# A series of 552 TensorE matmuls behind the last store of a one-layer decoder step

## The chip, the cores and the metric

The kernel runs on one core of a Trainium2 chip. The metric is the device time of one execution in microseconds (us). A program has five queues that matter here: TensorE (PE, with its weight loads shown apart as PEld), VectorE (DVE), ScalarE (ACT), GpSimd (POOL) and SyncE (SP). SP issues nearly all DMA transfers; ACT and POOL issue some.

## The reference, cut to what matters

One layer of a hybrid decoder is computed for 256 prompt tokens and 8 sample tokens, so 264 token columns in all, with a model width of 2048:

```
z  = rmsnorm(x) @ w_in                    # RG-LRU group and mLSTM group from one projection
x  = x + concat(y_rg, y_ml) @ w_out
x  = x + cross_attention(rmsnorm(x), memory K/V)
x  = x + (silu(xf @ w_gate) * (xf @ w_up)) @ w_down
y  = rmsnorm_final(x)
```

The outputs are y, the new recurrent states and the memory keys and values. All is float32.

## The kernel before

The token columns lie along the free axis (`N = 264`) and the model width along the partitions, in 16 chunks of 128 (`KC = 16`). A list `steps` holds the projections one after the other. For each step the weights are fetched by SP into a tile `raw` (128 x 1024), split by ACT and DVE into a high and a low part in float32r (tiles with the tag `w`, four buffers of `WW = 2176` columns), and multiplied on TensorE. Each product of 128 x 128 weights with 128 x 264 activations takes three matmuls (`mm3`: high by high, high by low, low by high), so that float32 accuracy comes from float32r matmuls. Their moving operands lie in tiles with the tag `B`, and every moving operand in the kernel is read over consecutive columns. The memory keys and values use 512- and 256-column matmuls of the same type. A few small matmuls (token sums, spreading a column, transposes) are done in plain float32; the profile shows each of those as two rows.

The activations in flight belong to generators that a planner advances between steps by estimated clocks; the order on SP is written out by hand, that of the other engines is set by a scheduler. None of that order is touched ahead of the final normalisation.

The end of the kernel is what the change and the prediction speak of. After the last down projection the sum of squares goes over DVE, ACT and PE; `rstd_fin` leaves the factor twice, once in a PSUM bank (read by DVE) and once copied by ACT into the tile `rstd` (read by POOL). Then 16 chunks of `y` are multiplied, 12 on DVE and the four of `POOLC = (4, 5, 10, 11)` on POOL, and stored in nine transfers, four issued by ACT and five by SP:

```python
    for lo, hi in ((0, 1), (1, 2), (2, 4), (4, 6), (6, 8), (8, 10), (10, 12), (12, 14), (14, 16)):
        for c in range(lo, hi):
            e, r = (pool_e, rstd) if c in POOLC else (dve, fin["ps"][:, :N])
            e.tensor_mul(st["y"](c), st["y"](c), r)
        (act if lo in (1, 4, 8, 12) else sp).dma_start(o_y[:, lo:hi, :], st["y"].tile(lo // 4)[:, lo % 4: lo % 4 + hi - lo, :])
```

`st["y"].tile(q)` is one of four `B` tiles that hold four chunks each. A PSUM tile (`bank()`) has 512 float32 columns. After these lines each queue waits at a barrier for the others, SP also for the landing of the stores, and the execution ends.

## Time and profile before

| | us |
|---|---|
| two timed runs | 1552.85 and 1553.53, median 1553.19 |
| span of the profiled execution, first to last instruction | 1548.1 |
| PE busy | 1533.5 (99%), 12098 instructions |
| PEld busy | 1500.4 (97%) |
| DVE busy | 1055.5 (68%) |
| ACT busy | 784.0 (51%) |
| mean granted TensorE clock | 0.997 |

The profile gives the span of the execution that it recorded; the time of a run contains what lies around the span, and the median is 5.1 us above it. The duration of one matmul in the profile is a latency: matmuls overlap, so that what one of them costs in a stream is the distance from one start to the next, which is got from a stretch of time and the number of matmuls in it.

### The profile page before, as it was taken

Reading aid. Unit: us, or ns where it says so; the run is one execution under the profiler, and the core shown is the slowest. Engines: PE = TensorE matmul, PEld = TensorE weight load, DVE = VectorE, ACT = ScalarE, POOL = GpSimd, SP = SyncE. Lnnn points to the kernel's source line nnn. Section 1 sums busy time; section 2 is a strip of 40 time slices with the busy share of each in tenths; the row PEclk is TensorE's granted clock in tenths of the full one; section 3 lists DMA queues with packets and bytes.
Section 4 is the critical chain, followed back from the end, with each engine's and each line's share of the span. In section 5 each row is a group of like instructions: output and inputs, shape, how many; then the busy total and the mean of one; then the engine's idle time right before and its main releaser. Section 6 shows DMA issues by size and latency. Waiting matters only on the chain.

```text
span 1548.1 us, 30188 instructions
## 1 busy us (share of the span) xinstructions
PE 1533.5 (99%) x12098; PEld 1500.4 (97%) x12098; DVE 1055.5 (68%) x2026; ACT 784.0 (51%) x1255; POOL 123.7 (8%) x190
## 2 busy tenths in 40 slices
PE   9999999999999999999999999999999999999997
PEld 9999999999999888899999999999999999999997
DVE  7886888796699989876665555445555545555554
ACT  7565775665455656555444444333444433444463
POOL 0001210000134333310000000000000000000000
PEclk9999999999999999999999999999999999999999
DMA  9556984547789887855555555555555555555563
GB/s 301 187 164 204 309 288 171 193 158 259 251 294 356 320 296 252 309 181 180 187 177 181 186 181 188 181 185 183 183 185 181 186 183 186 180 188 178 163 181 107
DMA packets 99757, 326.01 MB, mean 211 GB/s; under 512 B 10945, under 2 KB 19825, under 8 KB 99617
## 3 DMA queue, kind: packets, MB, share of 16 engines
q1 hardware_dynamic: 83472, 269.57, 52.1%
q0 software_dynamic: 15136, 53.16, 9.7%
q8 instruction: 94, 1.54, 0.4%
q10 hardware_dynamic: 1008, 1.36, 0.3%
q14 instruction: 47, 0.38, 0.1%
HBM read 312.78 MB, written 11.28 MB: 209 GB/s over the span
## 4 chain that ended last, share of the span: by engine, by line
PE 96%; DVE 2%; ACT 1%; DMA 0%; issue 0%; SPq 0%; DVEq 0%; ACTq 0%
PE mm L60 90%; PE ax L60 6%; DVE B L60 1%; ACT B L60 0%; DVE w L60 0%; DMA raw<-w_in 0%; ACT w L60 0%; ACT L60 0%; DVE xres L60 0%; DVE c L60 0%; ACT rstd L60 0%; SPq L1278 0%; DVE acc_x L60 0%; DVEq L1429 0%; ACT t L60 0%
## 5 line engine op out<-in xcount | busy, mean ns | idle before, releaser
L60 PE MATMUL mm<-B,w 128*128 128x264 f32 (+1 forms) x10960 | 1365.3, 285 | 4.1 <-DVE w L60 2.4
L60 PEld LDWEIGHTS mm<-B,w 128*128 128x128 f32 x10960 | 1338.6, 188 | 16.4 <-DVE w L60 2.8
L60 ACT ACTIVATE w<-raw 128x1024 fp32r<-128x1024 f32 (+1 forms) x522 | 537.9, 1031 | 654.6 <-PE mm L60 447.3
L60 DVE TENSOR_TENSOR w<-raw,w 128x1024 fp32r<-128x1024 f32 (+1 forms) x522 | 623.1, 1195 | 357.0 <-ACT w L60 356.0
L60 PE MATMUL mm<-w,B 128*128 128x512 f32 x384 | 91.0, 391 | 0.0
L60 PEld LDWEIGHTS mm<-w,B 128*128 128x128 f32 x384 | 70.7, 188 | 14.3
L60 DVE TENSOR_TENSOR t<-mm,rstd 128x264 f32<-128x264 f32 x104 | 44.8, 431 | 44.2 <-PE mm L60 43.5
L1344 POOL TENSOR_TENSOR B<-B,rstd 128x264 f32<-128x264 f32 x4 | 2.8, 736 | 855.5 <-ACT rstd L60 855.5
L60 DVE TENSOR_TENSOR xres<-xres,mm 128x264 f32<-128x264 f32 (+1 forms) x81 | 34.2, 423 | 38.9 <-PE mm L60 38.9
L60 DVE SCALAR_TENSOR_TENSOR B<-B,dw 128x256 f32<-128x256 f32 x128 | 55.6, 488 | 3.9 <-ACT dw L60 3.9
L60 DVE SCALAR_TENSOR_TENSOR dw<-B,qsm,dw 128x256 f32<-128x256 f32 x96 | 49.6, 525 | 0.4
L60 PE MATMUL ax<-B,B 128*128 128x256 f32 (+3 forms) x288 | 48.1, 308 | 0.0
L60 PEld LDWEIGHTS ax<-B,B 128*128 128x128 f32 x288 | 40.8, 190 | 3.2 <-ACT w L60 0.3
L1031 POOL TENSOR_TENSOR ds<-dw,ds 128x256 fp32r<-128x256 f32 x32 | 34.6, 1085 | 108.1 <-ACT ds L60 108.1
L60 ACT ACTIVATE B<-xres,vecs 128x264 fp32r<-128x264 f32 (+1 forms) x64 | 32.1, 502 | 1.5 <-DVE xres L60 1.0
L60 ACT ACTIVATE t<-xres 128x264 f32<-128x264 f32 (+2 forms) x61 | 24.0, 410 | 15.2 <-DVE xres L60 15.2
L1020 POOL DMA_DIRECT2D B<-kcT x32 | 17.3, 542 | 140.1 <-DVE B L60 131.0
L60 ACT ACTIVATE B<-t 128x264 fp32r<-128x264 f32 (+1 forms) x60 | 24.2, 409 | 4.6 <-DVE t L60 4.3
L60 DVE TENSOR_TENSOR acc_x<-acc_x,t 128x264 f32<-128x264 f32 x59 | 25.1, 426 | 1.0 <-ACT t L60 0.5
L60 DVE SCALAR_TENSOR_TENSOR B<-xres,vecs,B 128x264 fp32r<-128x264 f32 x48 | 23.4, 487 | 3.1 <-ACT B L60 3.1
L60 ACT ACTIVATE t<-t 128x264 f32<-128x264 f32 (+1 forms) x61 | 24.8, 406 | 1.3 <-DVE t L60 1.2
L60 ACT ACTIVATE dw<-B,qsm 128x256 f32<-128x256 f32 x32 | 16.2, 507 | 17.4 <-DVE B L60 10.7
(152 smaller groups left out, 666.9 us busy)
## 6 DMA issues: line engine op xcount, KB each, us to landing
raw<-w_gu SPq DMA_DIRECT2D x176, 512.0 KB, 3.5
raw<-w_d SPq DMA_DIRECT2D x80, 512.0 KB, 3.5
raw<-w_in SPq DMA_DIRECT2D x74, 512.0 KB, 4.6
raw<-w_out SPq DMA_DIRECT2D x32, 512.0 KB, 4.0
B<-kcT POOLq DMA_DIRECT2D x32, 512.0 KB, 8.1
raw<-w_q SPq DMA_DIRECT2D x32, 512.0 KB, 3.7
B<-vcT POOLq DMA_DIRECT2D x32, 512.0 KB, 8.5
raw<-w_k SPq DMA_DIRECT2D x32, 512.0 KB, 6.8
```

Source lines behind the costliest of these rows:

```text
L60: return f(*a, **k)
L1020: pool_e.dma_start(kc, kcT[h, b])
L1031: pool_e.tensor_sub(ws[:, 1], acc, ws[:, 0].bitcast(F32))
L1344: e.tensor_mul(st["y"](c), st["y"](c), r)
```

## The change

A function `probes` is added and called after the last store. It copies chunks of the finished `y` with ACT into three tiles of the tag `w`, and then lets TensorE run 23 forms of 24 matmuls each, 552 in all, with weights from the first tile (eight places in turn) and a moving operand from the second. The results go to one PSUM bank that nothing reads. The third tile is written and never read.

```diff
+    def probes(y):
+        RL = 24
+        wt = [sb.tile([P, WW], F32R, tag="w", bufs=4, name=nm("w")) for _ in range(3)]
+        for n, t in enumerate(wt):
+            for q in range(2):
+                act.activation(t[:, q * 1056: q * 1056 + 1056].rearrange("p (c n) -> p c n", n=N), y.tile(q + n % 2), AF.Copy)
+            act.activation(t[:, 2112:2176], y.tile(n)[:, 0, 0:64], AF.Copy)
+        banks = [bank() for _ in range(2)]
+        mm = nc.tensor.matmul
+        W_ = lambda k: wt[0][:, 264 * (k % 8): 264 * (k % 8) + P]
+        with tc.manual_schedule(engines={mybir.EngineType.PE}):
+            N2, W2 = [[1, 132], [132, 2]], [[1, 256], [256, 2]]
+            A2, E2 = [[2, 132], [1, 2]], [[2, 256], [1, 2]]
+            pat = [
+                ("plain", 0, [[1, 264]], None), ("plain", 0, [[1, 264]], None),
+                ("halves in turn, out plain", 0, N2, [[1, 264]]),
+                ("halves in turn, out by pairs", 0, N2, A2),
+                ("pairs, out plain", 0, A2, [[1, 264]]), ("pairs, out by pairs", 0, A2, A2),
+                ("backward pairs", 1, [[2, 132], [-1, 2]], [[1, 264]]),
+                ("halves in turn from 4", 4, N2, [[1, 264]]), ("halves in turn from 2", 2, N2, [[1, 264]]), ("halves in turn from 8", 8, N2, [[1, 264]]),
+                ("512 plain", 0, [[1, 512]], None), ("512 halves in turn, out plain", 0, W2, [[1, 512]]),
+                ("512 pairs", 0, E2, E2),
+                ("512 lines in turn", 0, [[1, 256], [1056, 2]], [[1, 512]]),
+                ("256 plain", 0, [[1, 256]], None), ("256 halves in turn", 0, [[1, 128], [128, 2]], [[1, 256]]),
+                ("128 plain", 0, [[1, 128]], None), ("128 halves in turn", 0, [[1, 64], [64, 2]], [[1, 128]]),
+                ("backward halves in turn", 131, [[-1, 132], [132, 2]], [[1, 264]]),
+                ("second half first", 132, [[1, 132], [-132, 2]], [[1, 264]]),
+                ("512 halves in turn in two groups", 0, [[256, 2], [1, 128], [128, 2]], [[1, 512]]),
+                ("two far lines in turn, 512", 0, [[1, 256], [1024, 2]], [[1, 512]]),
+                ("plain", 0, [[1, 264]], None),
+            ]
...
+            for name, o, ap, oap in pat:
+                x = AP(wt[1][:, o: o + 1], ap)
...
+                for k in range(RL):
+                    mm(out, W_(k), x, start=k == 0, stop=k == RL - 1, skip_group_check=True)
...
+    probes(st["y"])
```

A pattern is a list of pairs of a step and a count in columns of 4 bytes, the last pair running fastest: `[[1, 132], [132, 2]]` reads columns 0, 132, 1, 133, 2, 134 and so on, two streams in turn. The moving operand of a "pairs" form names its columns two by two, which is their plain order. All outputs are written to consecutive columns.

On TensorE the program ended with the spreading of the final factor (`ident` by the column `c`, into the bank `ax`); now the series follows it. `mm_17856` is the bank, `w_17845` the moving tile and `w_17844` the weights. The piece of TensorE's difference at the end of the program:

```order
 L60 MATMUL ax_17814<-ident,c_17798 128x128 x2
 L60 MATMUL ax_17814<-ident,c_17798 128x8
-L1429 UNCONDITIONAL_BRANCH
+L957 MATMUL mm_17856<-w_17845,w_17844 128x264 x240
+L957 MATMUL mm_17856<-w_17845,w_17844 128x512 x96
+L957 MATMUL mm_17856<-w_17845,w_17844 128x256 x48
+L957 MATMUL mm_17856<-w_17845,w_17844 128x128 x48
+L957 MATMUL mm_17856<-w_17845,w_17844 128x264 x48
+L957 MATMUL mm_17856<-w_17845,w_17844 128x512 x48
+L957 MATMUL mm_17856<-w_17845,w_17844 128x264 x24
+L1478 UNCONDITIONAL_BRANCH
```

Nothing on TensorE ahead of the series moved; 552 matmuls stand behind what used to be its last. The first of them waits for ACT's copies.

On ACT, the end of the program before, from the last small activation on (`B_17017`, `B_17227`, `B_17436` and `B_17645` are the four tiles of `y`):

```order
L60 ACTIVATE c_17798<-c_17797 128x3
L60 ACTIVATE rstd<-ax_17814 128x264
L1345 DMA o_y<-B_17017 128x264
L1345 DMA o_y<-B_17227 128x528
L1345 DMA o_y<-B_17436 128x528
L1345 DMA o_y<-B_17645 128x528
L1429 UNCONDITIONAL_BRANCH
```

And the same place with the change, up to the copy for which the first matmul of the series waits:

```order
L60 ACTIVATE c_17798<-c_17797 128x3
L60 ACTIVATE w_17844<-B_17017 128x64
L60 ACTIVATE rstd<-ax_17814 128x264
L1392 DMA o_y<-B_17017 128x264
L60 ACTIVATE w_17844<-B_17017 128x1056
L60 ACTIVATE w_17845<-B_17227 128x64
L1392 DMA o_y<-B_17227 128x528
L1392 DMA o_y<-B_17436 128x528
L1392 DMA o_y<-B_17645 128x528
L60 ACTIVATE w_17844<-B_17227 128x1056
L60 ACTIVATE w_17845<-B_17227 128x1056
```

One 64-column copy stands ahead of the copy of `rstd`, a 1056-column and a 64-column copy stand between ACT's first and second store, and the other copies behind ACT's last store. The first matmul of the series waits for the last row shown; behind it ACT has four more copies (`w_17845<-B_17436` and three into the third tile). DVE, POOL and SP keep their order.

More of the change, by code (lines that the diff above doesn't have):

```diff
@@ L907, in layer_kernel, with AP @@
         proj(w_in[33 + j], rx, evac_o(j))
+    def probes(y):
[20 more added lines that the diff above has]
+                ("512 pairs", 0, E2, E2),
[3 rows of a table added]
+                ("backward halves in turn", 131, [[-1, 132], [132, 2]], [[1, 264]]),
[4 more added lines that the diff above has]
+            ]
+            def AP(src, ap):
+                return bass.AP(src.tensor, src.offset, [list(src.ap[0])] + [list(q) for q in ap])
+            for name, o, ap, oap in pat:
+                x = AP(wt[1][:, o: o + 1], ap)
+                out = AP(banks[0][:, 0: 1], oap or ap)
+                if len(ap) == 2 and oap is not None and len(oap) == 1:
+                    out = AP(banks[0][:, 0: 1], oap).rearrange("p (a b) -> p a b", b=ap[-1][1])
+                if len(ap) == 3:
+                    out = banks[0].rearrange("p (a b c) -> p a b c", a=2, c=2)
+                for k in range(RL):
+                    mm(out, W_(k), x, start=k == 0, stop=k == RL - 1, skip_group_check=True)
```

## The prediction

> **What bounds the kernel now.** I read the shares by engine first, then the chain that ended last, then the end of the timeline.

> ```profile
> span 1548.1 us, 30188 instructions
> PE 1533.5 (99%) x12098; PEld 1500.4 (97%) x12098; DVE 1055.5 (68%) x2026; ACT 784.0 (51%) x1255; POOL 123.7 (8%) x190
> PE 96%; DVE 2%; ACT 1%; DMA 0%; issue 0%; SPq 0%; DVEq 0%; ACTq 0%
> ```

> TensorE sets the time of all stages but the last few microseconds. The change touches only that end, so the end is what has to be read:

> ```profile
> 1538.24 1.50 PE L60 MATMUL ax<-ident,c 128*128 128x128 f32 x12
> 1539.12 4.16 DVE L60 TENSOR_TENSOR B<-B,ax 128x264 f32<-128x264 f32 x12 [0.93 <-PE ax L60]
> 1539.57 4.73 SPq L1345 DMA_DIRECT2D o_y<-B  x5
> 1539.92 3.21 ACTq L1345 DMA_DIRECT2D o_y<-B  x4
> 1540.26 2.84 POOL L1344 TENSOR_TENSOR B<-B,rstd 128x264 f32<-128x264 f32 x4 [855.47 <-ACT rstd L60]
> o_y<-B SPq DMA_DIRECT2D x4, 264.0 KB, 2.6
> ```

> TensorE has its last work at 1538.24 and is done at 1539.74. DVE multiplies `y` until 1543.28, POOL until 1543.10, ACT has issued its stores by 1543.13 and SP its last one by 1544.30; with 2.6 us to landing that is 1546.9, and the span ends 1.2 us after it, the closing of the program. So 8 us of TensorE idleness stand at the end, and only stores run there.

> **The change part by part.** *What is added ahead of the series: ACT's copies.* The first matmul waits for the second 1056-column copy behind ACT's last store. Copies of nearly that width:

> ```profile
> L60 ACT ACTIVATE w<-raw 128x1024 fp32r<-128x1024 f32 x36 | 38.2, 1060 | 47.1 <-PE mm L60 19.8 <-issue 18.4 <-ACT B L60 8.8
> ```

> 1060 ns for 1024 columns makes 1.09 us for 1056 columns. ACT is free at 1543.13 as before: the copies put between its stores (one of 1056, two of 64 columns) fit into the time in which it waits for DVE and POOL, 1540.2 to 1542.6, so I cost them at nothing; without that cover they would cost 1.09 us and some 0.3 each for the small ones. The 64-column copy ahead of `rstd` holds up POOL by at most 0.3 us and with it SP's last two stores, which land long before the series ends; if POOL were late enough to hold up ACT's stores too, the series would start by as much later. Two copies from 1543.13 on bring **the first matmul at 1545.3**. At that moment the stores are still landing, and the four copies left on ACT (3 x 1.09 and a small one, until some 1549) run beside the series.

> *The series.* It has 144 matmuls of 264 columns read in plain order (three plain forms, two by pairs, one by backward pairs, which takes each pair of neighbours together), 48 of 512, 24 of 256 and 24 of 128 read so; and, read as two streams in turn, 168 of 264, 96 of 512, 24 of 256 and 24 of 128 columns. Plain pitches:

> ```profile
> 900.00:1000.00 100.00, 100.00 (x837) 100.00 (x836) 54.86 (x64) 40.27 (x46) 0.00 (x0) 1.00 0.55 185
> 566.91 5.40 PE L60 MATMUL mm<-w,B 128*128 128x512 f32 x23
> 589.25 1.12 PE L60 MATMUL ax<-B,B 128*128 128x256 f32 x8
> 1535.24 0.83 PE L60 MATMUL mm<-ones 128*128 128x128 f32 x6
> 1535.12 0.76 PEld L60 LDWEIGHTS mm<-ones 128*128 128x128 f32 x6
> ```

> The first row is 100 us of the down and up projections, all 264-column matmuls: 100 / 837 = 0.120 us each. In the others I take the latency of the last matmul off (means in the row groups below) and divide by the steps between starts: (5.40 - 0.39) / 22 = 0.228 us for 512 columns, (1.12 - 0.28) / 7 = 0.120 for 256, (0.83 - 0.27) / 5 = 0.112 for 128. The last agrees with the weight load, (0.76 - 0.19) / 5 = 0.114: a matmul of 128 columns is bound by its weights.

> ```profile
> L60 PE MATMUL mm<-w,B 128*128 128x512 f32 x384 | 91.0, 391 | 0.0
> L60 PE MATMUL ax<-B,B 128*128 128x256 f32 x216 | 33.9, 295 | 0.0
> L60 PE MATMUL mm<-B,w 128*128 128x264 f32 x10448 | 1272.4, 283 | 4.1 <-DVE w L60 2.4 <-DVE B L60 1.7
> ```

> Plain forms: 144 x 0.120 + 48 x 0.228 + 24 x 0.120 + 24 x 0.112 = **33.8 us**.

> [...]

> *The forms in turn* have no row: no matmul of the kernel before reads its moving operand with a step. Below stands the plain pitch, as if the order of reading cost nothing. Above I look for the slowest stream of columns in the trace, the plain float32 product, which is shown as two rows per matmul:

> ```profile
> 75.91 1.05 PE L60 MATMUL ax<-B,B 128*128 128x264 f32 x4
> L60 PE MATMUL ax<-B,B 128*128 128x264 f32 x32 | 8.4, 386 | 0.0
> ```

> (1.05 - 0.39) / 3 = 0.222 us for one row of 264 columns, two clock steps per column, and 0.444 for the product of two rows. These are my three prices per 264 columns: 0.120 below, 0.222 in the middle, 0.444 above. I take the middle one. A plain read finds the next column beside the last one, and a read in turn finds it 256 to 4224 bytes away every time; if the operand is fetched by more than one column at once, half of what is fetched is lost at the least, and two steps per column is the smallest whole number above one. In proportion to the columns: 168 x 0.222 + 96 x 0.431 + 24 x 0.215 + 24 x 0.112 (two steps for 128 columns just equal the weight load) = 37.3 + 41.3 + 5.2 + 2.7 = **86.5 us**. The backward pairs would add 24 x 0.102 = 2.4 us if they too went by halves.

> [...]

> *The clock.* After TensorE's last work the granted clock goes down, and it comes back in steps of 3.41 us:

> ```profile
> 122.31:125.72 3.41, 3.41 (x18) 3.41 (x17) 3.41 (x5) 0.30 (x2) 0.00 (x0) 0.50 0.60 185
> 1542.10:1542.25 0.15, 0.00 (x0) 0.00 (x0) 0.15 (x2) 0.00 (x0) 0.15 (x1) 1.00 1.18 437
> 1542.26:1548.00 5.74, 0.00 (x0) 0.00 (x0) 1.01 (x3) 0.00 (x0) 0.84 (x2) 0.50 0.72 275
> ```

> The drops at 122.31 and 1542.25 lie 416 x 3.413 us apart, as on a fixed grid. The next points of it are 1545.7 and 1549.1. The series starts inside the first of these intervals, so the full clock is back at 1549.1, after one wholly busy interval. From 1545.3 to 1549.1 half the work is done: **1.9 us** lost.

> *The end.* Behind the last matmul come its latency beyond its pitch (0.16 us) and the closing, 1.2 us as before: **1.4 us**. The stores have long landed.

> **Sum.** 1545.3 + 33.8 + 86.5 + 1.9 + 1.4 = 1668.9 us of span. The time lies 5.1 us above the span (1553.2 against 1548.1), so **1674 us**, +121 us or 7.8%. Nothing ahead of 1540 us is changed: the order on PE, DVE, POOL and SP is the same there.

> **The rivals.**

> *Reading in turn costs nothing.* The forms in turn go at the plain pitch: 168 x 0.120 + 96 x 0.228 + 24 x 0.120 + 24 x 0.112 = 47.7 us in place of 86.5, so 1674 - 38.8 = 1635 us. For it: in the plain rows TensorE takes 4 bytes per column at every step, and the 2.40 columns per ns between the 256- and the 512-column pitch ((512 - 256) / (0.228 - 0.120) = 2370 per us) show no limit of the fetch other than the array's own step. Against it: all these rows are of neighbours.

> *Only some addresses collide.* Streams 132 columns (528 bytes) apart go at the plain pitch, streams a multiple of 256 bytes apart at half of it: the 168 matmuls of 264 columns cost 20.2 us, the rest 49.2 as above, together 69.4: 1657 us. For it: the plain pitch is not quite even, and the kernel's tables lay weights and activations at fixed distances. Against it: no row here separates addresses.

> *Every column waits for its own fetch, four steps.* With 0.444 us per 264 columns: 74.6 + 82.7 + 10.3 + 5.2 = 172.8 us, so 1674 + 86.3 = 1760 us. For it: if one fetch brings four neighbouring columns, a read in turn uses a quarter of it. Against it: nothing in the trace streams that slowly.

> *The series is not run, or runs inside the end.* The results are unread, and every form begins anew in the same bank; if the matmuls were dropped ahead of execution, only ACT's copies would remain: five of 1.09 us and a small one from 1543.13 on, 1548.9, closing 1.2: span 1550.1, time 1555 us, within 2%. It decides from the point where 552 matmuls take less than 1548.1 + 31 - 1545.3 - 1.4 = 32 us, 59 ns each. Against it: the program's order for TensorE holds all 552, each with its own weights, and the trace has no pitch below the 0.112 of a weight load for any full-width matmul.

> **How the numbers follow.** A difference of 2% (31 us) is about what a measurement of this kernel can tell from no change. Chances: two steps per column 0.40, no cost 0.21, some addresses 0.13, four steps 0.22, not run 0.02, anything else 0.02. The ends of the unknown price are the first rival at 1635 and the four steps at 1760. Each holds about a fifth, so that neither can be left out together with the last two cases. With a few us for the uneven plain pitch the range is 1630 to 1765. All cases but one are slower by over 2%: slower 0.98, same 0.02, faster 0.

> **What would show it.** In the changed profile: the first matmul of line 957 at 1545.3 (right if within 0.7 us), behind a copy on ACT; a granted clock of 0.50 until 1549.1 and 1.00 after; the rows of the plain forms at 0.120 and 0.228 us; those in turn at 0.222 and 0.431 with 0.215 and 0.112 for the narrow ones; the backward pairs at 0.120; and 1.4 us between the last matmul's start and the end. The forecast is wrong if the forms in turn stand at any other pitch, or differ among each other; if plain forms in this layout (weights and moving operand in two like tiles) are slower than in the projections, the first term is mis-sized; and if TensorE is slower ahead of 1540 us, the change reaches further than I read it.

## The result, and the profile after

| | before | with the series |
|---|---|---|
| time, median | 1553.19 us | 1632.4 us (1631.46 and 1633.34) |
| ratio | | 1.0515 (95% interval 1.0496 to 1.0535) |
| span of the profiled execution | 1548.1 us | 1631.6 us |

The kernel is slower by 79 us, inside the range and in the direction forecast, but 42 us below the likeliest value. What happened is the first rival (1635 us), and a little more than it: reading two streams in turn does not cost twice the plain pitch, as the forecast had it; it is quicker than plain reading (0.1125 us for 264 columns against 0.121).

The page of the changed kernel; the last two rows are groups (line, engine, operation, count, busy time, mean latency, idle time before):

```profile
span 1631.6 us, 31303 instructions
PE 1616.7 (99%) x12650; PEld 1578.1 (97%) x12650; DVE 1055.1 (65%) x2026; ACT 790.3 (48%) x1264; POOL 125.1 (8%) x190
L957 PE MATMUL mm<-w,w 128*128 128x264 f32 (+3 forms) x552 | 80.7, 310 | 5.5 <-ACT w L60 5.5
L957 PEld LDWEIGHTS mm<-w,w 128*128 128x128 f32 x552 | 75.8, 192 | 10.4 <-ACT w L60 5.6
```

All 552 matmuls ran, so the case that they are dropped is out; together they took 80.7 us. The end of the timeline:

```profile
1542.55 1.50 PE L60 MATMUL ax<-ident,c 128*128 128x128 f32 x12
1543.42 4.17 DVE L60 TENSOR_TENSOR B<-B,ax 128x264 f32<-128x264 f32 x12 [0.93 <-PE ax L60]
1544.90 1.23 ACT L60 ACTIVATE w<-B 128x1056 fp32r<-128x1056 f32 x2 [0.42 <-DVE B L60]
1546.03 1.39 ACTq L1392 DMA_DIRECT2D o_y<-B  x3
1547.47 5.12 ACT L60 ACTIVATE w<-B 128x1056 fp32r<-128x1056 f32 x6 [1.34 <-POOL B L1391]
1549.58 80.74 PE L957 MATMUL mm<-w,w 128*128 128x264 f32 x552 [5.53 <-ACT w L60]
```

The first matmul of the series starts 7.03 us (1549.58 - 1542.55) after the first `ident` matmul; 7.06 had been forecast (1545.3 - 1538.24). It waits for ACT, as the row says.

Stretches of the series, each from the first matmul of one form to the first of the next (start and end, length, then busy time and count of PE, PEld, DVE, ACT, POOL, then the granted clock; the counts include the matmuls cut by the edges, 24 start in each). In order: the first plain form, the second, halves in turn, pairs, backward pairs, 512 plain, 512 halves in turn, 256 plain, 256 halves in turn:

```profile
1549.58:1553.92 4.34, 4.34 (x25) 4.34 (x25) 0.00 (x0) 3.02 (x4) 0.00 (x0) 0.66 0.26 94
1553.92:1556.82 2.90, 2.90 (x27) 2.90 (x25) 0.00 (x0) 0.00 (x0) 0.00 (x0) 1.00 0.00 0
1556.82:1559.52 2.70, 2.70 (x27) 2.70 (x25) 0.00 (x0) 0.00 (x0) 0.00 (x0) 1.00 0.00 0
1565.13:1568.03 2.90, 2.90 (x26) 2.90 (x25) 0.00 (x0) 0.00 (x0) 0.00 (x0) 1.00 0.02 6
1568.03:1570.95 2.92, 2.92 (x27) 2.92 (x25) 0.00 (x0) 0.00 (x0) 0.00 (x0) 1.00 0.00 0
1579.05:1584.66 5.61, 5.61 (x26) 4.51 (x25) 0.00 (x0) 0.00 (x0) 0.00 (x0) 1.00 0.02 3
1584.66:1589.84 5.18, 5.18 (x25) 4.53 (x24) 0.00 (x0) 0.00 (x0) 0.00 (x0) 1.00 0.00 0
1600.63:1603.45 2.82, 2.82 (x26) 2.81 (x24) 0.00 (x0) 0.00 (x0) 0.00 (x0) 1.00 0.00 0
1603.45:1606.12 2.67, 2.67 (x26) 2.67 (x25) 0.00 (x0) 0.00 (x0) 0.00 (x0) 1.00 0.00 0
```

Divided by 24: 264 columns take 0.121 us plain, by pairs and by backward pairs, and 0.1125 in turn; 512 columns 0.234 and 0.216; 256 columns 0.1175 and 0.111. The first form shows the half clock (0.50 until 1552.5): 4.34 in place of 2.91. All seven 264-column forms in turn, whatever column they start at and whichever half comes first, stand at 0.1125 (one of them is 0.06 us longer in all, at its first matmul), and all four 512-column ones at 0.216.

### The profile page after: what moved, and what is told of

Read it like the earlier page. It is cut to its first block, busy times and chain, and to the rows that moved or that the text cites. A ratio compares the mean times of both kernels' runs of the same rounds, so it can differ in the third digit from the quotient of the medians.

```text
span 1631.6 us, 31303 instructions
## 1 busy us (share of the span) xinstructions
PE 1616.7 (99%) x12650; PEld 1578.1 (97%) x12650; DVE 1055.1 (65%) x2026; ACT 790.3 (48%) x1264; POOL 125.1 (8%) x190
## 4 chain that ended last, share of the span: by engine, by line
PE 96%; DVE 2%; ACT 1%; DMA 0%; issue 0%; ACTq 0%; DVEq 0%; SPq 0%
PE mm L60 86%; PE ax L60 5%; PE mm L957 5%; DVE B L60 2%; DVE w L60 0%; ACT B L60 0%; DMA raw<-w_in 0%; ACT w L60 0%; ACT L60 0%; DVE t L60 0%; ACTq L1478 0%; DVE xres L60 0%; DVE c L60 0%; ACTq L1392 0%; ACT rstd L60 0%
## 5 line engine op out<-in xcount | busy, mean ns | idle before, releaser
L60 PE MATMUL mm<-B,w 128*128 128x264 f32 (+1 forms) x10960 | 1367.0, 285 | 4.1 <-DVE w L60 2.4
L60 PEld LDWEIGHTS mm<-B,w 128*128 128x128 f32 x10960 | 1340.3, 188 | 16.3 <-DVE w L60 2.8
L60 ACT ACTIVATE w<-raw 128x1024 fp32r<-128x1024 f32 (+1 forms) x522 | 537.9, 1031 | 658.0 <-PE mm L60 448.7
L60 DVE TENSOR_TENSOR w<-raw,w 128x1024 fp32r<-128x1024 f32 (+1 forms) x522 | 623.0, 1195 | 360.1 <-ACT w L60 359.3
L60 PE MATMUL mm<-w,B 128*128 128x512 f32 x384 | 91.0, 391 | 0.0
L957 PE MATMUL mm<-w,w 128*128 128x264 f32 (+3 forms) x552 | 80.7, 310 | 5.5 <-ACT w L60 5.5
L957 PEld LDWEIGHTS mm<-w,w 128*128 128x128 f32 x552 | 75.8, 192 | 10.4 <-ACT w L60 5.6
L60 PEld LDWEIGHTS mm<-w,B 128*128 128x128 f32 x384 | 70.7, 188 | 14.3
L60 DVE TENSOR_TENSOR t<-mm,rstd 128x264 f32<-128x264 f32 x104 | 44.9, 432 | 44.1 <-PE mm L60 43.5
L60 DVE TENSOR_TENSOR xres<-xres,mm 128x264 f32<-128x264 f32 (+1 forms) x81 | 34.4, 425 | 38.9 <-PE mm L60 38.9
L60 DVE SCALAR_TENSOR_TENSOR B<-B,dw 128x256 f32<-128x256 f32 x128 | 55.7, 490 | 3.9 <-ACT dw L60 3.9
L60 DVE SCALAR_TENSOR_TENSOR dw<-B,qsm,dw 128x256 f32<-128x256 f32 x96 | 49.8, 527 | 0.4
L60 PE MATMUL ax<-B,B 128*128 128x256 f32 (+3 forms) x288 | 48.4, 309 | 1.4 <-DVE B L60 1.4
L60 PEld LDWEIGHTS ax<-B,B 128*128 128x128 f32 x288 | 40.7, 190 | 5.0 <-DVE B L60 2.0
L60 ACT ACTIVATE B<-xres,vecs 128x264 fp32r<-128x264 f32 (+1 forms) x64 | 32.1, 502 | 1.5 <-DVE xres L60 1.0
L60 ACT ACTIVATE t<-xres 128x264 f32<-128x264 f32 (+2 forms) x61 | 24.0, 410 | 15.2 <-DVE xres L60 15.2
L60 ACT ACTIVATE B<-t 128x264 fp32r<-128x264 f32 (+1 forms) x60 | 24.2, 408 | 4.0 <-DVE t L60 3.8
L60 DVE TENSOR_TENSOR acc_x<-acc_x,t 128x264 f32<-128x264 f32 x59 | 25.4, 430 | 1.0 <-ACT t L60 0.5
L60 DVE SCALAR_TENSOR_TENSOR B<-xres,vecs,B 128x264 fp32r<-128x264 f32 x48 | 23.6, 492 | 3.1 <-ACT B L60 3.1
```

The source lines that it names most:

```text
L60: return f(*a, **k)
L957: mm(out, W_(k), x, start=k == 0, stop=k == RL - 1, skip_group_check=True)
```

## Experiments

Three questions were asked: is it the reading and nothing else that makes the difference; what in the reading; and does it hold where the other engines work.

**Copies only.** `pat` is empty; ACT's copies stay.

```diff
+            pat = []
             for name, o, ap, oap in pat:
```

> The changed kernel with the series left out, ACT's nine copies kept. If the series alone is what costs: 1555 us (ACT ends some 5.5 us later than before, the stores land as before). If the copies between ACT's stores hold up the end: more than 1560 us.

Measured 1553.27 us (one run; the kernel before on the same chip 1551.48, 1549.83 to 1553.73 in seven runs). The copies end the program here:

```profile
span 1551.5 us, 30199 instructions
1540.26 1.50 PE L60 MATMUL ax<-ident,c 128*128 128x128 f32 x12
1545.19 5.12 ACT L60 ACTIVATE w<-B 128x1056 fp32r<-128x1056 f32 x6 [1.35 <-POOL B L1392]
```

From the first `ident` matmul to the end of the span it is 11.24 us, against 9.86 before (1548.1 - 1538.24): the copies alone cost 1.4 us. The rest of the 79 us is the series.

**All forms plain.**

```diff
+            pat = [(n, 0, [[1, int(np.prod([q[1] for q in ap]))]], None) for n, o, ap, oap in pat]
```

> The changed kernel with every form read over consecutive columns, counts and widths kept. If reading in turn is what is quicker: the series from first to last start takes 312 x 0.121 + 144 x 0.234 + 48 x 0.117 + 48 x 0.111 = 82.4 us and 1.4 for the half clock, 83.8 where the changed kernel took 80.5; the time some 3 us above 1632.4. If the pitch depended on the place in the series and not on the reading: 80.5 again.

Measured 1635.58 us (one run). The series, its groups of 264 and 512 columns, and the stretches of the third and the twelfth form, which the changed kernel reads in turn:

```profile
1547.00 85.54 PE L958 MATMUL mm<-w,w 128*128 128x264 f32 x552 [5.53 <-ACT w L60]
L958 PE MATMUL mm<-w,w 128*128 128x264 f32 x312 | 41.2, 297 | 5.5 <-ACT w L60 5.5
L958 PE MATMUL mm<-w,w 128*128 128x512 f32 x144 | 34.0, 396 | 0.0
1555.67:1558.58 2.91, 2.91 (x27) 2.91 (x25) 0.00 (x0) 0.00 (x0) 0.00 (x0) 1.00 0.00 0
1584.56:1590.18 5.62, 5.62 (x26) 4.52 (x24) 0.00 (x0) 0.00 (x0) 0.00 (x0) 1.00 0.00 0
```

85.54 us against 80.74. More of this series fell into the half clock: its first two forms took 8.68 us in place of 5.82, a loss of 2.86, where the changed kernel lost 4.34 - 2.91 = 1.43. Without that loss it is 82.7 against 79.3, 3.4 us more; expected were 82.4 between first and last start, and 82.4 came out. At their places in the series the third form takes 2.91 us in place of 2.70 and the twelfth 5.62 in place of 5.18. So the forms in turn are quicker because of how they read (2.70 against 2.91 at the same place), not because of where they stand.

**Which reading is quick.** The series is replaced by 26 other forms; the 24 matmuls of a form, the tiles and the place stay. `w` chooses the weights.

```diff
+                ("plain, one weight column for all", 0, [[1, 264]], None, Wb),
...
+                ("runs of 2, out in runs of 2", 0, R2, R2, W_),
...
+                ("step 2, out plain", 0, [[1, 2], [2, 132]], [[132, 2], [1, 132]], W_),
...
+                ("in turn 4 apart, out plain", 0, [[8, 33], [1, 4], [4, 2]], [[8, 33], [2, 4], [1, 2]], W_),
...
-            for name, o, ap, oap in pat:
+            for name, o, ap, oap, w in pat:
```

`Wb` is one weight column given for all 128, `R2` runs of two columns from each half.

> The same place and length (24 matmuls a form, 26 forms), other forms; in the changed kernel 264 columns took 0.121 us read plainly and 0.1125 read as two streams in turn. Theory A, the moving operand's reads collide with the weight load that runs beside them, and reading in turn gives each fetch more time: with one weight column loaded for all 128 (step 0) the plain form goes to 0.1125 too, one moving column for all also; with weights always from the same place the plain pitch depends on the distance of the moving operand from it (0, 8, 16, 32, 64 columns), by some ns. Theory B, consecutive columns themselves are fetched too slowly, whatever the weights do: plain with one weight column stays at 0.121, and the distance changes nothing. Of the run length: if what counts is that two neighbouring columns never follow each other, runs of 2 from each half stay at 0.121 as the backward pairs did; if it is the time between two fetches from one place, runs of 2 and 4 go to 0.1125 and only long runs (12, 44) come back to 0.121. Steps of 2, 4, 8 and 32 columns: A and B both leave open, 0.1125 if a new line per column is free, 0.22 if it is not.

Measured 1642.01 us (one run); what matters are its stretches of 24 as above, in order: in turn; plain with the output in runs of 2; plain with one weight column for all; plain with the weights always from the same place; runs of 2 from each half; runs of 4; a step of 2; four streams in turn; in turn with the streams 4 columns apart.

```profile
1556.38:1559.08 2.70, 2.70 (x26) 2.70 (x25) 0.00 (x0) 0.00 (x0) 0.00 (x0) 1.00 0.00 0
1561.98:1564.89 2.91, 2.91 (x27) 2.91 (x25) 0.00 (x0) 0.00 (x0) 0.00 (x0) 1.00 0.00 0
1564.89:1567.77 2.88, 2.88 (x26) 2.88 (x25) 0.00 (x0) 0.00 (x0) 0.00 (x0) 1.00 0.02 6
1570.47:1573.39 2.92, 2.92 (x27) 2.92 (x25) 0.00 (x0) 0.00 (x0) 0.00 (x0) 1.00 0.00 0
1585.09:1589.16 4.07, 4.07 (x26) 4.07 (x25) 0.00 (x0) 0.00 (x0) 0.00 (x0) 1.00 0.00 0
1593.24:1596.34 3.10, 3.10 (x27) 3.10 (x26) 0.00 (x0) 0.00 (x0) 0.00 (x0) 1.00 0.00 0
1602.35:1608.01 5.66, 5.66 (x26) 4.97 (x25) 0.00 (x0) 0.00 (x0) 0.00 (x0) 1.00 0.00 0
1624.35:1627.76 3.41, 3.41 (x25) 3.41 (x24) 0.00 (x0) 0.00 (x0) 0.00 (x0) 1.00 0.02 5
1630.53:1633.23 2.70, 2.70 (x26) 2.70 (x25) 0.00 (x0) 0.00 (x0) 0.00 (x0) 1.00 0.00 0
```

Theory A falls: with one weight column for all the plain form stays at 0.120, and moving the operand by 8 to 64 columns against fixed weights changes it between 0.121 and 0.123 only. (Every form still loads its weights; no run leaves the load out.) Neither guess about the runs was right: runs of 2 are the slow ones (0.170), 4, 12 and 44 stand at 0.129, 0.127 and 0.124. It is the reading and not the output: a plain reading with the output in runs of 2 takes 0.121, runs of 2 with a plain output 0.170 as well. Steps of 2 and 4 columns cost 0.236 and 0.240 per 264, of 8 and 32 columns 0.219 and 0.222 per 256, where plain takes 0.1175. So a price near the forecast one (0.222 per 264, 0.215 per 256) exists, but it belongs to stepping and not to reading in turn. The difference between a step of 2 and "in turn 4 apart" gave the next question: in the second, the first columns of all pairs form a sequence 0, 1, 2, 3, 8 and so on, the second ones 4, 5, 6, 7, 12.

**Pairs.** The same frame; each form reads 132 pairs, `[step from pair to pair, 132], [distance in the pair, 2]`.

```diff
+                ("pairs 1 apart, moving on by 1", 0, [[1, 132], [1, 2]], A2, W_),
...
+                ("pairs 1056 apart, moving on by 2", 0, [[2, 132], [1056, 2]], A2, W_),
...
+                ("pairs 1056 apart, moving on by 4", 0, [[4, 132], [1056, 2]], A2, W_),
...
+                ("pairs 1 apart, moving on by 4", 0, [[4, 132], [1, 2]], A2, W_),
```

> Again the same place, 19 forms of 24. The last run left a pattern: 264 columns read in pairs from two streams took 0.1125 us with the streams 4, 12 or 132 columns apart, plain columns 0.121, steps of 2, 4, 8 columns 0.22 to 0.24. That fits an operand taken two columns at a time, the first ones of the pairs making one sequence and the second ones another. Theory H: each of the two sequences wants several of its columns from one piece of 16 bytes (4 columns), whatever the other does; plain has 2 per piece and sequence, in turn 4, a step of 2 or more 1. It expects: pairs 1 apart, 0 apart or 2 apart that move on by 1: 0.1125; pairs 1056 apart moving on by 2: 0.121; by 3: between; by 4 and 8: 0.22; pairs 1 apart moving on by 4 or 8: 0.22. Theory S: the two columns of a pair collide when they lie in the same piece, and a new piece costs nothing of itself. It expects: pairs 1, 0 and 2 apart moving on by 1: 0.121 (or worse); pairs 1056 apart moving on by 2, 4 and 8: 0.1125; pairs 1 apart moving on by 4 or 8: 0.121. 256 columns, streams 128 and 64 apart in place of 132 and 66: by H as before in proportion (0.165 for runs of 2, 0.138 for four streams); if banks by address mattered: other values.

Measured 1621.19 us (one run). In order: pairs 1 apart moving on by 1; pairs 1056 apart moving on by 2, by 3 and by 4; pairs 1 apart moving on by 4:

```profile
1558.70:1561.40 2.70, 2.70 (x27) 2.70 (x26) 0.00 (x0) 0.00 (x0) 0.00 (x0) 1.00 0.00 0
1572.20:1575.03 2.83, 2.83 (x27) 2.83 (x25) 0.00 (x0) 0.00 (x0) 0.00 (x0) 1.00 0.00 0
1575.03:1579.28 4.25, 4.25 (x27) 4.25 (x25) 0.00 (x0) 0.00 (x0) 0.00 (x0) 1.00 0.00 0
1579.28:1584.92 5.64, 5.64 (x25) 4.98 (x25) 0.00 (x0) 0.00 (x0) 0.00 (x0) 1.00 0.01 3
1590.69:1596.34 5.65, 5.65 (x25) 4.98 (x24) 0.00 (x0) 0.00 (x0) 0.00 (x0) 1.00 0.00 0
```

| pairs are apart by (columns) | and move on by | us per 264 columns | H expected | S expected |
|---|---|---|---|---|
| 0, 1, 2, 4, 132, 1056 | 1 | 0.1125 (all six) | 0.1125 | 0.121 for 0, 1, 2 |
| 1056 | 2 | 0.118 | 0.121 | 0.1125 |
| 1 (that is plain) | 2 | 0.121 | 0.121 | 0.121 |
| 1056 | 3 | 0.177 | between | 0.1125 |
| 1056 | 4, 8 | 0.235, 0.240 | 0.22 | 0.1125 |
| 1 | 4, 8 | 0.236, 0.240 | 0.22 | 0.121 |

The distance inside a pair hardly matters (0.118 against 0.121 at a step of 2, no difference at 1, 4 and 8), the step from pair to pair does. S falls; H holds in every row, within 0.02. (The step of 2 of the run before reads 0, 2, 4, 6: as pairs it moves on by 4, and its 0.236 is that of the last row.) Plain reading moves on by 2 from pair to pair and thus loses 7% against reading that moves on by 1 (0.121 against 0.1125 us).

The rows also give H its price. At steps of 2, 3 and 4 the 132 columns of a sequence lie in 66, 99 and 132 pieces of four columns, and 0.118, 0.177 and 0.235 us are 1.8 ns for each piece; at a step of 8 it is 132 pieces again, and 0.240. At a step of 1 the 33 pieces would make 0.059 by that price, less than the 0.1125 measured, so there something else sets the pace.

By the number of columns that each sequence takes from a piece the rows read: four 0.1125, two 0.118 to 0.121, which is 5 to 8% more, one 0.235. For the operand as a whole nearness does not decide: in turn every column lies 131 or 132 columns from the one before, and that form is quicker than plain (0.1125 against 0.121).

What H does not explain: when a sequence goes back and forth between two places (runs of 2: 0, 132, 2, 134; four streams: 0, 132, 1, 133), H would give the price of a new piece at each column (0.235, as at a step of 4), and 0.170 and 0.142 were measured. Runs of 4 and 12 (0.129 and 0.127) lie above the 0.121 that H gives them, and one pair 132 apart read over and over (a step of 0) takes 0.115, not 0.1125. With 128 and 64 columns in place of 132 and 66 it is 0.166 and 0.142 per 256 columns, where H's proportion of those rows had given 0.165 and 0.138, so these distances are not the cause. This stays open.

**Runs of 2 in the kernel itself.** No series; the moving operand and the output of `mm3` by two columns from each half in turn, so that nothing else has to change.

```diff
+    def turn(a):
+        return a.rearrange("p (b a c) -> p a b c", b=2, c=2)
     def mm3(ps, a, b, start, stop):
         ah, al = a
         bh, bl = b
+        ps, bh, bl = turn(ps), turn(bh), turn(bl)
```

> The kernel before, without any series; in the three-matmul products the moving operand is read by two columns from each half in turn (0 1, 132 133, 2 3, and so on) and the output is written in the same order, so that it stands as before. If runs of 2 have the quick pitch: some 10,700 matmuls by 0.0075 us less, 80 us, 1473 us. If runs of 2 are as slow as backward pairs were: 1553 us, the same. If the output in runs of 2 costs something: above 1553.

Measured 2086.68 us, ratio to the kernel before 1.3448 (1.3426 to 1.3471).

```profile
900.00:1000.00 100.00, 100.00 (x589) 100.00 (x588) 44.54 (x61) 34.90 (x49) 0.00 (x0) 1.00 0.39 129
```

100 / 589 = 0.170 us, the pitch that the form had in the series, where the output in runs of 2 cost nothing by itself (0.121 with a plain reading). Much slower as a version, and a first sign that a pitch from the series holds beside the work of the other engines.

**In turn in the kernel.** No series; operand and bank by single columns from two halves in turn, and DVE reads the bank back with a step of 2.

```diff
+    def turn(a):
+        return a.rearrange("p (b a) -> p a b", b=2)
+    def two(a):
+        return a.rearrange("p (b a) -> p b a", b=2)
+    def read(ps):
+        return ps.rearrange("p (a b) -> p b a", b=2)
+    def mm3t(ps, a, b, start, stop):
+        mm3(ps.rearrange("p (a b) -> p a b", b=2), a, (turn(b[0]), turn(b[1])), start, stop)
...
-            dve.tensor_add(x, x, ps[:, :N])
+            dve.tensor_add(two(x), two(x), read(ps[:, :N]))
```

> The kernel before, without any series; 9408 of its 10448 matmuls of 264 columns (32 projections of w_in, w_out, the attention's output, gate, up and down) read the moving operand as two streams 132 columns apart in turn, write it in that order, and DVE reads the bank back with a step of 2 columns, so that all tiles keep their order. If the quick pitch holds beside the work of the other engines: 9408 x (0.1195 - 0.1125) = 66 us less, 1486 us. If DVE's reading of the bank with a step costs much: less gain, up to none where DVE is the bound (480 to 720 us is not touched). If the quick pitch only holds where the other engines rest: 1552 us.

Measured 1491.14 us against 1551.69 on the same chip, ratio 0.961 (0.9593 to 0.9627). A stretch of the feed-forward stage, and two of DVE's groups that read the bank, followed by the same two groups before:

```profile
900.00:1000.00 100.00, 100.00 (x891) 100.00 (x891) 56.74 (x65) 41.40 (x44) 0.00 (x0) 1.00 0.58 196
L60 DVE TENSOR_TENSOR t<-mm,rstd 128x264 f32<-128x264 f32 x104 | 44.8, 431 | 28.8 <-PE mm L60 28.6
L60 DVE TENSOR_TENSOR xres<-xres,mm 128x264 f32<-128x264 f32 x79 | 33.7, 427 | 24.9 <-PE mm L60 24.8
L60 DVE TENSOR_TENSOR t<-mm,rstd 128x264 f32<-128x264 f32 x104 | 44.8, 431 | 44.2 <-PE mm L60 43.5 <-issue 0.2
L60 DVE TENSOR_TENSOR xres<-xres,mm 128x264 f32<-128x264 f32 x79 | 33.7, 427 | 35.3 <-PE mm L60 35.3
```

100 / 891 = 0.112 us. DVE takes 431 and 427 ns, and took 431 and 427 before: its reading of the bank with a step of 2 costs nothing. The gain is 60.5 us of the 66 expected. TensorE's busy time did fall by 65.2 us (1533.5 to 1468.3), but in the first 480 us of the profiled execution it waits 10.0 us in place of 5.9, for DVE and ACT; that is most of what is missing.

**More in turn.** Also the query projection, the memory keys and the memory values.

```diff
-            pe.matmul(ps, wh, rm(c), start=c == 0, stop=c == KC - 1, skip_group_check=True)
...
+            x = rm(c).rearrange("p (g b a) -> p g a b", g=2, b=2)
+            o = ps.rearrange("p (g a b) -> p g a b", g=2, b=2)
+            pe.matmul(o, wh, x, start=c == 0, stop=c == KC - 1, skip_group_check=True)
...
-                    pe.matmul(ps, mh[:, s], wh, start=(kc == 0), stop=False)
+                    pe.matmul(ps, mh[:, s], turn(wh), start=(kc == 0), stop=False)
```

> The version with 9408 matmuls read in turn (1491 us), and also the query projection (768 of 264 columns), the memory keys (256 of 512 columns in two groups of 256, 256 of 256) and the memory values (384 of 512) in turn; ACT and DVE read those banks with a step, DVE has one small instruction more per query step. If TensorE bounds these stages: 768 x 0.007 + 640 x 0.012 (from 0.228 to 0.216) + 256 x 0.006 = 15 us less, 1476 us. If DVE or the transfers bound them (DVE is busy 0.86 of the time between 480 and 720 us): 1486 to 1491 us. If ACT's reading with a step costs more than plainly: above 1491.

Measured 1474.43 us against 1550.14, ratio 0.95 (0.9477 to 0.9523). The last row is ACT's copy out of the bank before:

```profile
480.00:720.00 240.00, 240.00 (x1593) 224.59 (x1592) 211.47 (x500) 149.10 (x284) 66.63 (x87) 1.00 0.75 272
L60 PE MATMUL mm<-w,B 128*128 128x512 f32 x384 | 86.6, 380 | 0.0
L60 ACT ACTIVATE t<-mm 128x256 f32<-128x256 f32 x16 | 5.9, 367 | 0.0
L60 ACT ACTIVATE t<-mm 128x256 f32<-128x256 f32 x16 | 6.0, 372 | 0.0
```

The version before it ran on another chip; each against the kernel before on its own chip, the gains are 75.7 and 60.5 us, so 15.2 us more, 15 expected. TensorE, busy all of these 240 us, bounds the stage, although DVE is busy 0.88 of it. The 384 matmuls of the values went from 91.0 to 86.6 us, ACT's copies out of the bank with a step from 372 to 367 ns. This version beats both kernels of this case.

## Why the prediction was right or wrong

- **Direction: right**, for the reason given, and shared by every rival but the one in which the series is not run. The series stands on the path that sets the end, nothing covers it, and the copies alone cost 1.4 us.
- **Range: kept by luck.** 1632.4 us lies 2.4 us above its lower end. With the terms as measured, 1545.3 + 34.1 + 45.0 + 1.4 + 1.4 us make 1627.2 us of span, and with the 1.7 us around it 1628.9, below the range; the 4.3 us by which the end came later in this execution (below) carried the time in.
- **First matmul: right** by what it waits for, 7.03 us behind the start of the last spreading against 7.06; by the profile's time it came at 1549.58, not 1545.3, as the spreading itself was late. The copies between ACT's stores fitted into its waits: ACT has issued its last store 4.87 us after the first `ident` matmul, 4.89 before.
- **Plain forms: right.** 33.8 us forecast from the rows of before; measured 34.1 without the half clock (six forms of 264 columns at 2.91, two of 512 at 5.61, 2.82 and 2.63). The backward pairs, counted as plain by the estimate that they take each pair of neighbours together, took 2.92 us against 2.91.
- **Two small readings of the prediction do not hold.** Its sum took a latency of 0.28 us off the eight 256-column matmuls where the row shown has 295 ns; with 0.295 the pitch is 0.118 in place of 0.120, which the series bears out (0.1175). And the 2370 columns per us between two plain widths (printed there as 2.40 per ns, too) are not the pace of plain reading in the series: (512 - 256) / (0.234 - 0.1175) = 2200 there. No row of before gives 2.40 per ns or the array's own step; the prediction's clock steps per column are an estimate, 0.222 / 264 = 0.84 ns against 1 / 2370 us = 0.42 ns.
- **Forms in turn: wrong.** This is the step that failed, by the sign that the prediction itself had named (any other pitch than 0.222 and 0.431): 86.5 us forecast, 45.0 measured (seven forms at 2.70 and 0.06 once, four at 5.18, two at 2.68). I took the middle of three prices with the argument that a read in turn loses half of what is fetched at once; that was an estimate, and no run shows how much is fetched at once. The pairs show that the argument was about the wrong neighbour: for streams that move one way, what counts is not whether the next column lies beside the last one but whether the next-but-one does (0.1125 us when it does, whatever the distance in the pair; 0.235 when it lies four columns on). In turn it does, at every column. The lower bound was a bound by assumption only; the true price lay under it, 45.0 against the 47.7 of the first rival, because the plain reading itself has a loss that I had seen as an uneven pitch and not priced.
- **Clock: half right.** Half speed lasts until a point of the grid of 3.41 us, as forecast (a granted clock of 0.50 from 1545.68 to 1552.51, two steps of it), but no wholly busy interval was needed. The interval in which the series begins, first of the changed kernel, then of the all-plain series with the interval behind it:

```profile
1549.09:1552.51 3.42, 2.93 (x13) 2.93 (x14) 0.00 (x0) 3.42 (x5) 0.00 (x0) 0.50 0.47 173
1546.33:1549.75 3.42, 2.75 (x12) 2.76 (x13) 0.00 (x0) 3.42 (x4) 0.00 (x0) 0.50 0.52 195
1549.75:1553.16 3.41, 3.41 (x18) 3.41 (x17) 0.00 (x0) 0.26 (x2) 0.00 (x0) 0.50 0.00 0
```

An interval of which TensorE was busy 2.93 us brought the full clock back at its end; one with 2.75 us did not, and cost another interval. That is why the changed kernel lost 1.4 us and the all-plain one 2.9. By the rule of the prediction the changed kernel would have stayed at half speed until 1555.92 and lost 3.2 us, so that 1.4 lies near the forecast 1.9 by chance.
- **What lies around the span: mis-sized.** I put the profiled span (1548.1) against the median (1553.19) and carried 5.1 us. A later run of the kernel before had a span of 1548.1 and a time of 1549.83, and the changed kernel 1631.6 and 1633.34: 1.7 us lie around the span. The other 3.4 us are the difference between the profiled execution and the two timed ones.
- **Nothing ahead of the end: not quite as seen.** The first `ident` matmul came 4.3 us later. The rows of 120 to 240 us, first of before, then of the changed kernel, show where:

```profile
120.00:240.00 120.00, 118.48 (x932) 115.53 (x933) 95.59 (x280) 76.06 (x172) 20.84 (x39) 0.99 0.85 276
120.00:240.00 120.00, 117.00 (x900) 113.20 (x898) 93.24 (x278) 73.98 (x169) 20.84 (x39) 0.97 0.83 269
```

There are 32 matmuls fewer in the stretch (3.8 us at 0.120). In part it is a second drop of the clock in the mLSTM stage (0.97 in place of 0.99), in part waits: TensorE is busy 1.5 us less. In the profiles of the experiments with a series and of the copies the same point lies between 1539.96 and 1541.96, and seven runs of the kernel before spread over 3.9 us, so I put it down to the execution and not to the change; no run was made to separate the two. This 4.3 and the 3.4 of the item above nearly cancel, by chance.

## What to carry to other kernels

A price that no row of the profile shows should not be settled by a story about the fetch; both ends of the range were assumptions, the choice between them was not supported, and a form in a series of 24 matmuls would have told it in 3 us. A matmul's float32r operand of 256 columns or more is worth trying as two streams in turn, if its bank can be read back with a step: here that took 5% off a kernel whose TensorE was busy 99% of the time; with 128 columns, where the rows of before put the weight load (0.114 us) at the pitch of the matmul (0.112), nothing was gained (0.110 us plain, 0.111 in turn). A busy engine is not an engine at its peak: 264 columns in 0.120 us are 2200 per us, while the step from 264 to 512 columns read in turn, (512 - 264) / (0.216 - 0.1125), makes 2400.
